# A mixture-of-experts layer on one core: no zero fill of the table of rows, its sums before the last up-projection, and seven output banks begun ahead

## Chip, cores and metric

The kernel runs on one core of a Trainium2 chip. The metric is the device time of one execution in microseconds (us). The core has five engines with queues of their own: TensorE (PE in the profile; PEld is its weight load), VectorE (DVE), ScalarE (ACT), GpSimd (POOL) and SyncE (SP), which here only issues transfers (DMAs). ACT and POOL issue DMAs too; such an instruction stands in the engine's own program, in order with its computing instructions.

## The reference

One transformer layer over 512 latent tokens of width 1024, beside 256 context tokens: a mixer (neighbourhood attention and a gated delta net), then a mixture of 32 experts of which each token uses 4, then a final norm. The part that the change touches is the last:

```python
logits = xf @ w_router + b_router
top_val, top_idx = lax.top_k(logits, 4)
gates = softmax(top_val)
# for each token and each of its four experts e:
hb = x @ w1[e] + b1[e];  gate, up = hb[:1024], hb[1024:]
gate = min(gate, 7);  up = clip(up, -7, 7)
act = (up + 1) * gate * sigmoid(1.702 * gate)
y[token] += gates[token, e] * (act @ w2[e] + b2[e])
# then
out = rmsnorm(x1 + g2 * y, final_norm_w)
```

## The kernel before, in words

**Stages.** The first stage, the mixer, lasts to about 745 us. Its instructions are ordered by a scheduler that plans with a model of the times. PE multiplies in three products of split operands (`hh`, `hl` with `whi`, `wlo`), which ACT and DVE make from each weight block: ACT writes the rounded part `whi` (L29) and DVE the remainder `wlo` (L30). The weight blocks of the mixer are loaded by ACT's own queue (L1050). The delta net's part of it (L1380 to L1600) makes a triangular matrix per block (`AT`, L1413), sends it through memory (L1420, L1456), inverts it on DVE in 30 small steps (L1462, L1463), merges halves on PE (L1491, L1500, with `X` copied by ACT between them, L1493) and then runs 12 steps in a row (`step`); other projections fill PE between the steps.

**Experts.** The second stage takes the 32 experts in an order by their number of tokens. From `e = 2` on, every engine keeps the order of the program (`strict`). Expert `e` has gate weights `g`, up weights `u` and down weights `w2`, each as four chunks of 1 MB, and SP loads them in the order of `Stream.order`: `g` of `e`, `w2` of `e - 1`, `u` of `e`. Ten buffers (`RAWB`) hold the chunks; a chunk is asked for when the chunk ten places ahead of it has been used (`pump`). So all of this stage hangs on one stream of 384 chunks, and of eight more of kind `y`.

**Table of rows.** The weighted result of each expert (`weighted`) is written to the table `y4d` of 2048 rows (512 tokens, four slots each) by a scatter that POOL issues (`scatter`, L591). This is done for experts 0 to 29. Experts 30 and 31, both small (at most 64 tokens), never go through the table: `last(t, n, i)` adds them from `yl[i]` by a product with a 0/1 matrix. Rows of slots that belong to experts 30 and 31, or to tokens over an expert's capacity, must read as zero, so nine transfers on ACT's queue write zeros to the whole table in the mixer (L1434 to L1438), behind the stores of `v`.

**The end.** The table is read back as eight `y` chunks, two for each quarter `t` of the tokens; `rows_of(t)` adds them to the residual `x1`: one add on POOL and three on DVE for each `t`. In the stream they stand as four (quarters 0, 1) ahead of the last `u` and four (quarters 2, 3) ahead of the last `w2`. The output has eight banks (`t`, `n`), each a sum of four products on PE: `second` (bias), `last` with `i = 0` (expert 30), `rest` (`x1` times the identity) and `last` with `i = 1` (expert 31). Seven banks get the first two ahead of the last `w2` and `rest` between its third and fourth chunk; the eighth bank (3, 1) shares its room with the result of `w2` and is made after it. Then come the squares (ACT), the norm's factor (DVE), the scaling and four stores on SP's queue. Last stands a branch (`overflow`) for tokens over capacity, which is not entered with these inputs.

Of the kernel before, what the change touches and what calls it, by code (L numbers as in the profile page):

```python
# [38 lines left out]
class Stream:  # L39
# [3 lines left out]
    def __init__(self, tc, ctx, w1, w2, y4d, NE):  # L43
        self.tc, self.nc = tc, tc.nc
        self.pool = ctx.enter_context(tc.tile_pool(name="moe_raw", bufs=RAWB, side="right"))
        self.w1, self.w2, self.y4d = w1, w2, y4d
        self.raw = {}
        self.order = []
        for e in range(NE + 1):
            if e < NE:  # L50
                self.order += [(e, "g", c) for c in range(4)]
            if e:
                self.order += [(e - 1, "w2", c) for c in range(4)]
            if e < NE:
                self.order += [(e, "u", c) for c in range(4)]
        for i, t in ((-4, 2), (-12, 0)):
            self.order[i:i] = [(t + c // 2, "y", c % 2) for c in range(4)]
        self.loaded = self.used = 0
        self.eidx = None
        self.reg = {}  # L60
# [83 lines left out]
def moe(tc, ctx, cst, release, rps, rt, rtp, h2, hx, h2d, x1d, y4d, modd, w1, b1, w2, b2, fn_d, out, NE=32):  # L144
# [100 lines left out]
    def turn(e, src, q, dst):  # L245

        p = bank("tr").rearrange("p (k s) -> p k s", k=4)
# [9 lines left out]
    def turned(e, src, dst):  # L257
        for q in range(1 if small(e) else 2):
            turn(e, src, q, dst)
# [41 lines left out]
    tlast = sb.tile([128, 2, 4], F32, name="tlast")  # L301
    fnb = sb.tile([128, 1024], F32, name="fnb")
# [255 lines left out]
    GS, AT, TA, YS = {}, {}, {}, []  # L558
# [20 lines left out]
    def transp(e):  # L579
# [3 lines left out]
        turned(e, AT.pop(e), [t])  # L583
        TA[e] = [t]

    def scatter(e, y):
# [6 lines left out]
        for q in YS:  # L593
            tc.declare_no_dep(s.ins, q.ins, reason="rows of other slots")
        YS.append(s)
# [8 lines left out]
    def overflow(n, ovi, rowd, gatd):  # L604

        with tc.If(n > 0):
            with tc.For_i(0, n) as j:
                e = nc.values_load(ovi[0:1, bass.ds(j, 1)], min_val=0, max_val=31)
                with ExitStack() as s2:
# [56 lines left out]
                    tf = lp.tile([128, 4], F32, name="tf")  # L666
                    nc.vector.tensor_copy(tf[:, 0:1], tk)
                    for t in range(1, 4):
                        nc.vector.tensor_scalar(tf[:, t:t + 1], tf[:, 0:1], -128.0 * t, None, op0=OP.add)
                    ot = lp.tile([128, 4, 128], F32, name="ot")  # L670
                    for t in range(4):
                        nc.vector.tensor_scalar(ot[:, t], iot, tf[:, t:t + 1], None, op0=OP.is_equal)
                        for i in range(2):
                            p = bank("y")
                            v = slice(512 * i, 512 * i + 512)
                            nc.tensor.matmul(p, ot[:, t], y[:, v], start=True, stop=True)
                            nc.vector.tensor_tensor(x1[:, t, v], x1[:, t, v], p, op=OP.add)
# [3 lines left out]
    def second(t, n):  # L681
        LP[t, n] = bank(("h", "h", "tr", "y")[t])
        PE.matmul(LP[t, n], Gt[:, 128 * t:128 * t + 128], bs[:, 512 * n:512 * n + 512], start=True, stop=False)
# [6 lines left out]
    def rest(t, n):  # L690
        PE.matmul(LP[t, n], ident, x1[:, t, 512 * n:512 * n + 512], start=False, stop=False)
# [7 lines left out]

    for e in range(NE + 1):  # L700
        strict[0] = e >= 2
# [40 lines left out]
        if e:  # L742
# [5 lines left out]
            else:  # L748
                weighted(e - 1, p, yl[0])
                turned_()  # L750
                for t in range(2):
                    rows_of(t)
        nxt = e + 2 if 1 <= e < NE - 2 else None
        pu = mm(XT.pop(e), e, "u", (lambda c: gather(nxt) if c == 1 else None) if nxt else None)
        ahead(e + 1, "g")
        up(e, pu)
        if 1 <= e and e + 4 < NE:
            fetch(e + 4)

    transp(NE - 1)  # L760
    for t in range(2, 4):
        rows_of(t)
    p = [bank("y")]
    seven = [(t, n) for t in range(4) for n in range(2)][:7]
    for q in seven:
        second(*q)
        last(*q, 0)

    def early(c):
        if c == 2:  # L770
            for q in seven:
                rest(*q)

    p = mm(TA.pop(NE - 1), NE - 1, "w2", early, p)
# [70 lines left out]
def consts(tc, ctx):  # L845
# [15 lines left out]
    c["zero"] = zr = sb.tile([128, 120], F32, name="zero")  # L861
    nc.gpsimd.memset(zr, 0.0)
# [52 lines left out]
def mixer(tc, ctx0, ctx, ctx2, cst, I, rope_d, mask_d, modd, x1d, h2d, y4d, rt, dbg=None, upto=99):  # L915
# [1053 lines left out]
```

## Time and profile before

| | us |
|---|---|
| median of 3 runs (least, most) | 1869.85 (1867.04, 1880.26) |
| the profiled execution | 1870.34 |
| its span | 1868.5 |
| PE busy (share of the span) | 1701.3 (91%) |
| DVE busy | 986.8 (53%) |
| ACT busy | 623.6 (33%) |
| POOL busy | 272.9 (15%) |
| mean rate of the DMAs | 308 GB/s |
| zeros to the table | 8 transfers of 1020 KB and one of 32 KB |

The profiled execution lies 0.5 us above the median, and 1.8 us of its time lie around the span. The share of busy time is a mean over stages with different limits, so the rows are read stage by stage. A matmul's end is modelled, so the distance between starts tells more than its duration. In a timeline, neighbouring instructions of one kind are merged, with their count behind an x; in brackets stands how long the engine was idle ahead and what ended it.

### The profile page before, as it was taken

The numbers are of one execution on the slowest core, as the hardware profiler recorded it, in microseconds if no ns is written. First come the engines' busy times: TensorE is split into PE (matmuls) and PEld (weight loads), VectorE is DVE, ScalarE is ACT, GpSimd is POOL, SyncE is SP. The second block draws the span as 40 slices with busy tenths as digits, with TensorE's granted clock in tenths as the row PEclk, the third lists the DMA queues.
The fourth block names the chain that finished last, engine by engine and source line by source line (L and its number), as shares of the span: only waits on it lengthen the run. The fifth ranks groups of instructions, "written<-read, shape, count | busy, mean of one in ns | idle before, by whom it ended". The sixth has DMA issues, their size and how long they took to land. (4 is left out here: it accounts for less than half of the span.)

```text
span 1868.5 us, 25316 instructions
## 1 busy us (share of the span) xinstructions
PE 1701.3 (91%) x9475; PEld 1047.0 (56%) x9475; DVE 986.8 (53%) x1562; ACT 623.6 (33%) x851; POOL 272.9 (15%) x257
## 2 busy tenths in 40 slices
PE   5979896699999989789999999999999999999966
PEld 1556674587877768435455446554455645554412
DVE  2456792694556685834345337453354633553434
ACT  2534443333335542113224225232233432342201
POOL 0132100233200151310111011010110101100011
PEclk9989998799999999899999999999999999999989
DMA  7647749767488652999999999999999999999993
GB/s 254 206 128 225 212 117 269 204 161 181 134 201 210 190 180 102 351 366 409 410 409 409 409 408 408 399 398 402 408 398 402 400 384 409 405 409 383 410 410 134
DMA packets 280995, 574.68 MB, mean 308 GB/s; under 512 B 79150, under 2 KB 142082, under 8 KB 280740
## 3 DMA queue, kind: packets, MB, share of 16 engines
q1 hardware_dynamic: 185576, 488.25, 70.3%
q10 hardware_dynamic: 88237, 67.88, 12.8%
q0 software_dynamic: 7056, 16.91, 2.4%
q8 instruction: 76, 1.25, 0.3%
q14 instruction: 50, 0.41, 0.1%
HBM read 529.68 MB, written 51.02 MB: 311 GB/s over the span
## 5 line engine op out<-in xcount | busy, mean ns | idle before, releaser
L170 DVE TENSOR_TENSOR B<-raw,whi 128x2048 fp32r<-128x2048 f32 x120 | 273.5, 2290 | 170.6 <-ACT whi L170 170.3
L170 PE MATMUL y<-raw,at 128*64 128x512 f32 (+1 forms) x1024 | 336.7, 594 | 3.7 <-DMA raw<-in_w_dram 3.7
L170 ACT ACTIVATE whi<-raw 128x2048 fp32r<-128x2048 f32 x120 | 229.3, 1915 | 151.0 <-DMA raw<-in_w_dram 111.3
L170 PE MATMUL h<-raw,xts 128*64 128x512 f32 x1024 | 238.6, 608 | 13.7 <-DMA raw<-in_w_dram 13.6
L170 PEld LDWEIGHTS y<-raw,at 128*64 128x64 f32 (+1 forms) x1024 | 132.3, 163 | 190.3 <-issue 182.6
L1067 PE MATMUL pj<-hh,whi 128*128 128x512 f32 (+3 forms) x432 | 164.9, 384 | 21.7 <-ACT whi L29 16.9
L591 POOL DMA_INDIRECT y4d<-yy,rows x30 | 50.3, 1676 | 813.9 <-DVE yy L170 755.4
L170 DVE TENSOR_SCALAR h<-h 128x512 f32<-128x512 f32 x96 | 65.0, 694 | 184.6 <-PE h L170 184.6
L1068 PE MATMUL pj<-hl,whi 128*128 128x512 f32 (+3 forms) x432 | 161.0, 376 | 0.0
L1070 PE MATMUL pj<-hh,wlo 128*128 128x512 f32 (+3 forms) x432 | 159.1, 377 | 0.3 <-DVE wlo L30 0.3
L170 PEld LDWEIGHTS h<-raw,xts 128*64 128x64 f32 x1024 | 68.9, 139 | 151.0 <-issue 132.7
L170 PE MATMUL h<-whi,xth 128*128 128x512 f32 x480 | 137.1, 407 | 10.3 <-ACT whi L170 10.1
L170 PE MATMUL h<-B,xth 128*128 128x512 f32 x480 | 133.3, 399 | 6.1 <-DVE B L170 5.8
L170 PE MATMUL h<-whi,xtl 128*128 128x512 f32 x480 | 131.3, 395 | 0.0
L29 ACT ACTIVATE whi<-raw 128x512 fp32r<-128x512 f32 (+1 forms) x105 | 64.9, 625 | 183.3 <-PE pj L1068 83.2
L30 DVE TENSOR_TENSOR wlo<-raw,whi 128x512 fp32r<-128x512 f32 (+1 forms) x105 | 77.3, 741 | 90.5 <-ACT whi L29 90.3
L170 PEld LDWEIGHTS h<-whi,xth 128*128 128x128 f32 x480 | 86.3, 188 | 41.7 <-ACT whi L170 24.8
L170 PEld LDWEIGHTS h<-B,xth 128*128 128x128 f32 x480 | 87.9, 188 | 37.1 <-DVE B L170 18.0
L1067 PEld LDWEIGHTS pj<-hh,whi 128*128 128x128 f32 (+1 forms) x432 | 82.5, 191 | 46.8 <-ACT whi L29 18.2
L170 DVE SCALAR_TENSOR_TENSOR yy<-y,gates,g2b 128x512 f32<-128x512 f32 x32 | 24.0, 751 | 157.3 <-PE y L170 155.6
L170 ACT ACTIVATE at<-tr 128x512 f32<-128x512 f32 x48 | 27.0, 596 | 236.7 <-PE tr L170 236.7
L170 PEld LDWEIGHTS h<-whi,xtl 128*128 128x128 f32 x480 | 90.1, 188 | 21.7
(494 smaller groups left out, 2405.7 us busy)
## 6 DMA issues: line engine op xcount, KB each, us to landing
raw<-in_w_dram SPq DMA_DIRECT2D x384, 1024.0 KB
raw<-in_w_in_dram ACTq DMA_DIRECT2D x44, 512.0 KB
raw<-in_w_mod_dram ACTq DMA_DIRECT2D x32, 512.0 KB
raw<-in_w_mod_dram SPq DMA_DIRECT2D x16, 512.0 KB
raw<-y4d SPq DMA_DIRECT2D x8, 1024.0 KB
y4d<-zero ACTq DMA_DIRECT2D x8, 1020.0 KB
kk<-nkd SPq DMA_DIRECT2D x16, 384.0 KB
gad<-st ACTq DMA_DIRECT2D x16, 256.0 KB
```

Of the source, the lines that this page charges most:

```text
L29: nc.scalar.activation(hi, src, AF.Copy)
L30: nc.vector.tensor_tensor(lo, src, hi.bitcast(F32), op=OP.subtract)
L170: i = f(*a, **k)
L591: s = nc.gpsimd.indirect_dma_start(out=dst, out_offset=bass.IndirectOffsetOnAxis(ap=rows[:, k:k + 1], axis=0), in_=y, in_offset=None, boun ...
L1067: nc.tensor.matmul(p, h, mh(k), start=k == 0, stop=False)
L1068: nc.tensor.matmul(p, h, ml(k), start=False, stop=False)
L1070: nc.tensor.matmul(p, l, mh(k), start=False, stop=k == kb - 1)
```

## The change

Four things. The nine zero writes of the mixer go, and with them their order behind the stores of `v`. In their place POOL issues two scatters of a tile of zeros (128 x 512, set once) at the end of iteration `e = 3`, to the rows of experts 30 and 31. After the output, POOL scatters the two experts' results to the table, so that the overflow branch finds all rows there and makes its sums anew; the eight copies of the banks to `x1` at the end go. All eight `y` chunks stand ahead of the last `u`, and all four `rows_of` with them. The banks are begun in another order: four (`first`) get `second` and `last` with `i = 0` ahead of the last `u` and `rest` behind it; three (`then`) get all three products between `u` and `w2`; the eighth is summed in the room of `w2`'s result ahead of it and is kept as `x1` by an ACT copy.

```diff
-        for i, t in ((-4, 2), (-12, 0)):
-            self.order[i:i] = [(t + c // 2, "y", c % 2) for c in range(4)]
+        self.order[-8:-8] = [(t, "y", c) for t in range(4) for c in range(2)]
...
+    zero = sb.tile([128, 512], F32, name="zero")
+    nc.gpsimd.memset(zero, 0.0)
...
-        for q in YS:
+        for q in YS + (ZS if e < NE - 2 or zero else []):
             tc.declare_no_dep(s.ins, q.ins, reason="rows of other slots")
-        YS.append(s)
+        (ZS if zero else YS).append(s)
...
+    first, then = [(0, 0), (0, 1), (2, 0), (3, 0)], [(1, 0), (1, 1), (2, 1)]
...
                 weighted(e - 1, p, yl[0])
                 turned_()
-                for t in range(2):
+                pu, pt, pl = [bank("h")], bank("tr"), [bank("y")]
+                for q in first:
+                    second(*q)
+                    last(*q, 0)
+                for t in range(4):
                     rows_of(t)
...
+        if e == 3:
+            for i in range(2):
+                scatter(NE - 2 + i, zero, True)
...
-    transp(NE - 1)
-    for t in range(2, 4):
-        rows_of(t)
-    p = [bank("y")]
-    seven = [(t, n) for t in range(4) for n in range(2)][:7]
-    for q in seven:
+    for q in first:
+        rest(*q)
+    transp(NE - 1, pt)
+    for q in then:
         second(*q)
         last(*q, 0)
-    def early(c):
-        if c == 2:
-            for q in seven:
-                rest(*q)
-    p = mm(TA.pop(NE - 1), NE - 1, "w2", early, p)
+        rest(*q)
+    second(3, 1, pl[0])
+    last(3, 1, 0)
+    rest(3, 1, stop=True)
+    ACT.activation(x1[:, 3, 512:1024], pl[0], AF.Copy)
+    p = mm(TA.pop(NE - 1), NE - 1, "w2", None, pl)
     weighted(NE - 1, p, yl[1])
...
-    for q in seven:
+    for q in sorted(first + then):
         last(*q, 1)
-    second(3, 1)
-    last(3, 1, 0)
-    rest(3, 1)
+    rest(3, 1, start=True)
     last(3, 1, 1)
...
-    for (t, n), p in LP.items():
-        if n:
-            ACT.activation(x1[:, t, 512 * n:512 * n + 512], p, AF.Copy)
-        else:
-            DVE.tensor_copy(x1[:, t, 512 * n:512 * n + 512], p)
+    for i in range(2):
+        scatter(NE - 2 + i, yl[i])
...
-        d = nc.scalar.dma_start(vd[128 * t:128 * t + 128], v)
-        for i in range(2 * t, min(2 * t + 2, 9)):
-            z = cst["zero"][:, None, :].to_broadcast([128, 17, 120]) if i < 8 else cst["zero"][:, 0:64]
-            z = nc.scalar.dma_start(dap(y4d, i * 2040, [[16384, 128], [120, 17], [1, 120]] if i < 8 else [[16384, 128], [1, 64]]), z)
-            issue_behind(tc, z.ins, d.ins)
+        nc.scalar.dma_start(vd[128 * t:128 * t + 128], v)
```

Lines behind the diff's places shift by a few: the helper's L170 becomes L169, L591 becomes L592, L1493 becomes L1488.

On ACT, in the mixer where four of the zero writes stood (`vd` is the store of `v`, `whi` the rounded weights that PE waits for), before:

```order
L1378 DMA dgd<-st 128x512
L1433 DMA vd<-v 128x512
L1437 DMA y4d<-zero 128x17x120 x2
L1433 DMA vd<-v 128x512
L1437 DMA y4d<-zero 128x17x120 x2
L29 ACTIVATE whi<-raw 128x512 x2
L1357 ACTIVATE st<-pj 128x512
L1050 DMA raw<-in_w_in_dram 128x4x256
```

and now:

```order
L1378 DMA dgd<-st 128x512
L1433 DMA vd<-v 128x512
L1491 COPY T<-Z 32x8x32
L1492 COPY T<-Z 32x8x32
L1491 COPY T<-Z 32x8x32
L1492 COPY T<-Z 32x8x32
L1433 DMA vd<-v 128x512
L29 ACTIVATE whi<-raw 128x512
L1050 DMA raw<-in_w_in_dram 128x4x256
```

The four zero writes between the two `vd` stores and the next `whi` are gone; four copies of the merge have moved up in their place.

On PE, from the `w2` of expert 30 (`y<-raw`, its result banks) to the `u` of expert 31 (`h<-raw`); `h<-B`, `tr<-B`, `y<-B` are `second`, and `yl,oh` is `last`. Before:

```order
L170 MATMUL y<-raw,at 64x512 x16
L170 MATMUL tr<-ident,xtl 96x128 x4
L170 MATMUL h<-raw,xts 64x512 x16
L170 MATMUL h<-bb,bsel 128x512
L170 MATMUL tr<-ident,sg 128x128 x4
L170 MATMUL h<-B 128x512
```

and now:

```order
L169 MATMUL tr<-ident,xtl 96x128 x4
L169 MATMUL h<-B 128x512
L169 MATMUL h<-yl,oh 128x512
L169 MATMUL h<-B 128x512
L169 MATMUL h<-yl,oh 128x512
L169 MATMUL tr<-B 128x512
L169 MATMUL tr<-yl,oh 128x512
L169 MATMUL y<-B 128x512
L169 MATMUL y<-yl,oh 128x512
L169 MATMUL h<-raw,xts 64x512 x16
```

Four pairs of `second` and `last` now stand ahead of `u`.

On PE, from the last bank begun to the end (`y<-raw` is now the `w2` of expert 31, `A,ident` is `rest`). Before:

```order
L170 MATMUL y<-yl,oh 128x512
L170 MATMUL y<-raw,at 64x512 x12
L170 MATMUL h<-A,ident 128x512 x4
L170 MATMUL tr<-A,ident 128x512 x2
L170 MATMUL y<-A,ident 128x512
L170 MATMUL y<-raw,at 64x512 x4
L170 MATMUL h<-yl,oh 128x512 x4
L170 MATMUL tr<-yl,oh 128x512 x2
L170 MATMUL y<-yl,oh 128x512
L170 MATMUL y<-B 128x512
```

and now:

```order
L169 MATMUL y<-B 128x512
L169 MATMUL y<-yl,oh 128x512
L169 MATMUL y<-A,ident 128x512
L169 MATMUL y<-raw,at 64x512 x16
L169 MATMUL h<-yl,oh 128x512 x4
L169 MATMUL tr<-yl,oh 128x512 x2
L169 MATMUL y<-yl,oh 128x512
L169 MATMUL y<-A,ident 128x512
L169 MATMUL y<-yl,oh 128x512
```

The seven `rest` products have left `w2`, and behind it the eighth bank needs two products in place of four. On SP, three of the four output stores now stand behind the overflow branch; all four stood ahead of it.

## Rows read from the trace of the kernel before

**Rows 1.** Page, part 2: the whole span in 40 slices of 46.7 us

```profile
PE   5979896699999989789999999999999999999966
...
DMA  7647749767488652999999999999999999999993
GB/s 254 206 128 225 212 117 269 204 161 181 134 201 210 190 180 102 351 366 409 410 409 409 409 408 408 399 398 402 408 398 402 400 384 409 405 409 383 410 410 134
```

**Rows 2.** Busy time by stretch: PE, PEld, DVE, ACT, POOL, PEclk, DMA share, GB/s

```profile
300.00:310.00 10.00, 3.89 (x78) 2.82 (x76) 0.00 (x0) 2.21 (x5) 0.00 (x0) 0.99 1.10 270
310.00:320.00 10.00, 0.00 (x0) 0.00 (x0) 0.00 (x0) 0.00 (x0) 0.00 (x0) 0.50 1.16 287
...
340.00:350.00 10.00, 7.37 (x84) 6.05 (x85) 2.37 (x5) 3.11 (x7) 1.85 (x2) 0.63 1.00 250
```

**Rows 3.** Timeline, ACT and its queue: start, us, operation [idle before]

```profile
284.25 0.33 ACTq L1378 DMA_DIRECT2D dgd<-st  x1
...
305.18 6.06 ACTq L1437 DMA_DIRECT2D y4d<-zero  x2
311.34 3.93 ACTq L1433 DMA_DIRECT2D vd<-v  x1
315.31 5.30 ACTq L1437 DMA_DIRECT2D y4d<-zero  x2
320.66 1.15 ACT L29 ACTIVATE whi<-raw 128x512 fp32r<-128x512 f32 x2 [17.65 <-DMA vd<-v]
...
335.62 4.87 ACTq L1437 DMA_DIRECT2D y4d<-zero  x2
```

**Rows 4.** Timeline, PE, in the same stretch

```profile
321.35 0.79 PE L1067 MATMUL pj<-hh,whi 128*128 128x512 f32 x1 [16.21 <-ACT whi L29]
...
322.36 0.63 PE L1070 MATMUL pj<-hh,wlo 128*128 128x512 f32 x1
...
327.47 0.40 PE L1067 MATMUL pj<-hh,whi 128*128 128x512 f32 x1
...
342.63 0.26 PE L1500 MATMUL dn<-Z,X 32*32 32x32 f32 x2 [8.84 <-ACT X L1493]
...
360.53 0.43 PE L1565 MATMUL sc<-Sbd,KQ 128*64 128x128 f32 x2 [2.38 <-POOL KQ L1556]
```

**Rows 5.** Busy time by stretch, as in rows 2: filler, experts, last loads

```profile
430.00:745.00 315.00, 292.63 (x2590) 233.53 (x2591) 192.47 (x400) 130.25 (x246) 65.84 (x54) 0.99 0.63 173
757.00:1828.00 1071.00, 1025.90 (x4100) 543.38 (x4100) 508.25 (x544) 318.31 (x288) 127.54 (x74) 0.99 1.02 402
1828.00:1840.00 12.00, 12.00 (x38) 3.87 (x39) 5.92 (x4) 0.00 (x0) 2.70 (x1) 1.00 0.33 132
```

**Rows 6.** Timeline, SP: the four output stores

```profile
1853.54 8.29 SPq L802 DMA_DIRECT2D out_dram<-xf  x4
```

**Rows 7.** Timeline, PE, at the end

```profile
1797.42 1.94 PE L170 MATMUL y<-raw,at 128*64 128x512 f32 x8 [0.64 <-DMA raw<-in_w_dram]
...
1810.93 7.39 PE L170 MATMUL h<-raw,xts 128*64 128x512 f32 x24 [11.01 <-DMA raw<-in_w_dram]
...
1820.48 0.50 PE L170 MATMUL h<-bb,bsel 128*128 128x512 f32 x1
...
1822.97 0.48 PE L170 MATMUL h<-B 96*128 96x512 f32 x1
...
1833.32 5.37 PE L170 MATMUL y<-raw,at 128*64 128x512 f32 x24
1838.62 3.70 PE L170 MATMUL h<-A,ident 128*128 128x512 f32 x8
```

**Rows 8.** Timeline, DVE and ACT, at the end

```profile
1846.82 0.75 DVE L170 SCALAR_TENSOR_TENSOR yl<-y,gates,g2s 128x512 f32<-128x512 f32 x1 [12.77 <-PE y L170]
...
1855.01 0.60 ACT L170 ACTIVATE junk<-y 128x512 f32<-128x512 f32 x1 [2.07 <-PEq L606]
```

**Rows 9.** Table of rows: its scatters (ns least, median, most; first and last start)

```profile
L591 POOL DMA_INDIRECT y4d<-yy,rows x30: 989/1018/2825, 832.4 to 1773.0; - x30
```

More of the change, by code (lines that the diff above doesn't have):

```diff
@@ L243, in parts, with turn @@
         DVE.tensor_tensor(lo, src, hi.bitcast(F32), op=OP.subtract)
-    def turn(e, src, q, dst):
-        p = bank("tr").rearrange("p (k s) -> p k s", k=4)
+    def turn(e, src, q, dst, p=None):
+        p = (bank("tr") if p is None else p).rearrange("p (k s) -> p k s", k=4)
         for k in range(4):
@@ L255, in turn, with turned @@
             ACT.activation(dst[0][:, 4 * q:4 * q + 4], p, AF.Copy)
-    def turned(e, src, dst):
+    def turned(e, src, dst, p=None):
         for q in range(1 if small(e) else 2):
-            turn(e, src, q, dst)
+            turn(e, src, q, dst, p)
     def gather(e, src=None):
@@ L556, in mm @@
         return p
-    GS, AT, TA, YS = {}, {}, {}, []
+    GS, AT, TA, YS, ZS = {}, {}, {}, [], []
     def gate(e, p):
@@ L577, in up, with transp @@
         AT[e] = s
-    def transp(e):
+    def transp(e, p=None):
         t = wk3.tile([128, 8, 128], F32, name="at", bufs=2)
@@ L582, in transp, with scatter @@
             t = t[:, 0:4].rearrange("p a (b s) -> p (a b) s", b=2)
-        turned(e, AT.pop(e), [t])
+        turned(e, AT.pop(e), [t], p)
         TA[e] = [t]
-    def scatter(e, y):
+    def scatter(e, y, zero=False):
         k = column(e)
@@ L665, in overflow, with second @@
                         nc.vector.scalar_tensor_tensor(y[:, v], p, ga, g2b[:, v], op0=OP.mult, op1=OP.mult)
[L666 to L677, printed above, removed]
+                    nc.gpsimd.indirect_dma_start(out=y4d[:, :], out_offset=bass.IndirectOffsetOnAxis(ap=rw[:, 0:1], axis=0),
+                                                 in_=y, in_offset=None, bounds_check=2047, oob_is_err=False)
     LP = {}
-    def second(t, n):
-        LP[t, n] = bank(("h", "h", "tr", "y")[t])
-        PE.matmul(LP[t, n], Gt[:, 128 * t:128 * t + 128], bs[:, 512 * n:512 * n + 512], start=True, stop=False)
+    def second(t, n, p=None, stop=False):
+        LP[t, n] = p = bank(("h", "h", "tr", "y")[t]) if p is None else p
+        PE.matmul(p, Gt[:, 128 * t:128 * t + 128], bs[:, 512 * n:512 * n + 512], start=True, stop=stop)
     def last(t, n, i):
@@ L688, in last, with rest @@
         PE.matmul(LP[t, n], ohT[i][h, t, :], yl[i][h, :], start=False, stop=i == 1)
-    def rest(t, n):
-        PE.matmul(LP[t, n], ident, x1[:, t, 512 * n:512 * n + 512], start=False, stop=False)
+    def rest(t, n, start=False, stop=False):
+        PE.matmul(LP[t, n], ident, x1[:, t, 512 * n:512 * n + 512], start=start, stop=stop)
     def rows_of(t):
@@ L698, in rows_of @@
         stream.pump()
+    first, then = [(0, 0), (0, 1), (2, 0), (3, 0)], [(1, 0), (1, 1), (2, 1)]
     for e in range(NE + 1):
+        pu = None
         strict[0] = e >= 2
@@ L750, in moe @@
                 turned_()
-                for t in range(2):
+                pu, pt, pl = [bank("h")], bank("tr"), [bank("y")]
[3 more added lines that the diff above has]
+                for t in range(4):
                     rows_of(t)
         nxt = e + 2 if 1 <= e < NE - 2 else None
-        pu = mm(XT.pop(e), e, "u", (lambda c: gather(nxt) if c == 1 else None) if nxt else None)
+        pu = mm(XT.pop(e), e, "u", (lambda c: gather(nxt) if c == 1 else None) if nxt else None, pu)
         ahead(e + 1, "g")
@@ L833, in moe @@
     with tc.If(ovt[0] > 0):
+        nc.sync.dma_start(x1, x1d.rearrange("(t p) d -> p t d", p=128))
         for t in range(4):
+            for k in range(4):
+                r = stream.pool.tile([128, 2, 1024], F32, name="raw")[:, 0]
+                nc.sync.dma_start(r, y4d[512 * t + 128 * k:512 * t + 128 * k + 128, :])
+                nc.vector.tensor_tensor(x1[:, t], x1[:, t], r, op=OP.add)
+            for n in range(2):
+                p, v = bank("h"), slice(512 * n, 512 * n + 512)
+                nc.tensor.matmul(p, Gt[:, 128 * t:128 * t + 128], bs[:, v], start=True, stop=True)
+                nc.vector.tensor_tensor(x1[:, t, v], x1[:, t, v], p, op=OP.add)
             squares(t, [x1[:, t, 512 * n:512 * n + 512] for n in range(2)])
@@ L860, in consts @@
     nc.vector.memset(o1, 1.0)
-    c["zero"] = zr = sb.tile([128, 120], F32, name="zero")
-    nc.gpsimd.memset(zr, 0.0)
     c["sb"] = sb
```

## The prediction, made before the changed kernel ran

> **What bounds the kernel now.** I read the page's 40 slices first, because the kernel has two stages with different limits [rows 1]. From the 17th slice on the DMAs are busy for 9 tenths or more and move about 400 GB/s: that is the stream of expert weights. Ahead of it they move 102 to 269 GB/s, and PE has 9s and 8s with a hole in the 7th slice (a 6). Then I read busy time by stretch. From 757 to 1828 us the DMA share is 1.02 at 402 GB/s [rows 5]: the experts wait for their weights, so this stage ends a fixed time after its stream starts. In the mixer from 430 to 745 us PE is busy for 292.63 of 315 us [rows 5]: there PE is the limit, and what PE gains earlier passes through to the start of the stream. So two places decide: the mixer's hole, and what follows the last load.
>
> The hole is at 300 to 350 us. PE is idle for all of 310 to 320 us while the DMA share stands at 1.16 [rows 2]. The timelines say why. ACT needs 6.06 us to issue two zero writes, 3.93 us for a store of `v` behind them and 5.30 us for two more zero writes; only then, at 320.66, it makes the `whi` that PE has waited 16.21 us for [rows 3, 4]. An issue of the same queue took 0.33 us at 284 us [rows 3]. At 335.62 the last two zero writes hold ACT for 4.87 us, and PE waits 8.84 us for `X` [rows 3, 4]. At both places ACT has computing to do that stands behind an issue.
>
> At the end PE, not the stream, is last. The DMA share falls to 0.33 from 1828 to 1840 us while PE is busy throughout [rows 5]. PE had idled 11.01 us ahead of the last `u`, since four `y` chunks pass in front of it [rows 7].
>
> **The zero writes go.** I build the gain M of the mixer from four terms.
>
> A: PE's 16.21 us, less the 1.15 us of the two `whi` that ACT must make anyway [rows 3, 4]: 15.1 us. Bounds: 11.4 us if only the zeros' own issues (6.06 + 5.30) come back, 16.2 if the `whi` are ready in time.
>
> B: of the 8.84 us, the 4.87 us of issue, since the rest is the copies and the `X` that stand behind it: 4.8 us. Bounds 0 and 8.8.
>
> C: the clock. After the first gap the products from 321.35 us on, ten of them, show 0.63 us each (one row of them stands), against 0.40 at 327.47 [rows 4]; the granted clock in the gap was 0.50 [rows 2], which is 1.2 GHz. After the second gap eight more show 0.63. 18 × 0.2 = 3.6 us (rounding 0.23 down, as matmuls overlap). Bounds 0 and 4.1.
>
> D: loads of the first delta net steps come behind the zeros: from 340 to 350 us the DMA share is still 1.00 [rows 2], and PE waits for the load-fed `KQ` at 360.53, 2.38 us [rows 4]. I take those 2.4 us; the bounds are 0 and 7, three waits of that size.
>
> M = 15.1 + 4.8 + 3.6 + 2.4 = 25.9 us, bounds 11.4 and 36.1.
>
> The Trainium skill says on the page "DMA: Bandwidth & Descriptors", section "Issuing engines are not separate DMA queues", that issuing from several engines saves only the sequencer's time of issue, "which is usually small relative to the DMA itself". By that the ACT program would get back little, and the trace does not agree at this place: issues behind a full queue took 3 us each. The rival that the rule makes is the third below.
>
> The scheduler plans the mixer anew without the zeros, and the rows on ACT show four copies pulled ahead. That order has no price in the trace; I count it at nothing, with a few us either way inside the bounds of M.
>
> **The stream.** All eight `y` chunks and the four `u` and `w2` chunks are the same bytes as before. New are two scatters of at most 64 rows of 4 KB each, 0.52 MB at 402 GB/s [rows 5]: 1.3 us at most. POOL's issue costs 0.99 to 2.83 us each [rows 9] and lies beside the stream; behind them on POOL stand only gathers for four experts later. I take 1.3 us.
>
> **The end.** Four chunks more pass ahead of the last `u`: 4.19 MB at 402 GB/s are 10.4 us [rows 5]. Before, `u` ends at 1820.48 + 0.50 = 1820.98 [rows 7], and the last square starts at 1855.01 [rows 8], 34.0 us later. Let me count this distance anew, with prices from rows 7. A pair `second`, `last` costs 1.48 us (seven pairs from 1822.97 to 1833.32). A `rest` costs 0.9 us (eight halves, four products, in 3.70). A chunk of `w2` costs 1.8 us (three in 5.37). Now, behind `u`:
>
> - `rest` of four banks: 3.6
> - transposes: 0.4
> - three banks of 1.48 + 0.9: 7.1
> - the eighth bank: 2.4
> - its ACT copy, which `w2` waits for since it takes the same bank: 0.6 as the square of this size [rows 8] and 0.2 for the hand-over: 0.8
> - `w2`, all landed by then: 7.2
> - `yl` on DVE: 0.8 [rows 8]
> - from `yl` to the last square, before 1855.01 − 1847.57 = 7.4 [rows 8], now without one pair: 5.9
>
> The sum is 28.2 us, so PE wins 5.8 us and loses 10.4 us: the end comes 4.6 us later. DVE's wait for `u`, `up`, is hidden behind the four `rest`. The four sums `rows_of` run while PE waits for `u`; their last chunk lands four chunks ahead of `u`'s last. The four early pairs (5.9 us) lie in the wait ahead of `u`, which grows from 11.01 us by 10.4. PE restarts there at the low clock as it does now (24 products in 7.39 us, against 5.37 at full speed [rows 7]), so that loss stands on both sides. Bounds of the end: +2 (no hand-over and half of the bytes ahead) to +9 (the low clock lasts through `u` and the first `rest`).
>
> The scatter of `yl[0]` is issued by POOL behind its last add and puts 0.26 MB beside the last loads: 0.65 us at most, of which I count none, as PE is behind the loads. That of `yl[1]` runs beside the tail; POOL's scaling behind it starts 10 us later. Without the eight copies DVE and ACT stop earlier, but the stores end last. Three of the four stores now stand behind the branch on SP: the first store starts at 1853.54 and the four take 8.29 us [rows 6], so the branch has some 5 us in which the next tile is not ready. If that cover were gone, it costs at most the 6.7 us from the last store's issue (1861.83) to the span's end (1868.5), in which the branch lies now.
>
> **Sum.** 1870.34 (the profiled execution, 1.8 us of it around the span and 0.5 above the median) − 25.9 + 1.3 + 4.6 = 1850.3. I say 1850.
>
> **Rivals.**
>
> 1. *Everything in the hole comes back.* M = 36.1. For it: DVE shows no work at all from 300 to 320 us and ACT 2.21 us [rows 2], so neither would be the next limit there. Against: the other DMAs of this stretch must then fit into less time. 1870.3 − 36.1 + 5.9 = 1840.
>
> 2. *Only the zeros' own issues come back.* M = 11.4 to 16; the second wait, the loads and the clock stay because other loads crowd the queue. 1870.3 − 14 + 5.9 = 1862.
>
> 3. *The other side: ACT stays held.* If the 16.21 us hang on the `vd` stores and weight loads and not on the zeros, as the profile's own releaser ("DMA vd<-v") has it, ACT's queue is still full, or the lead is lost to the next wait. With M below 5.9 the change is slower; with M = 2 the time is 1874. Against: the eight large zero writes are 8.2 MB, where the whole 7th slice moved 12.6 MB (269 GB/s for 46.7 us [rows 1]), and an issue took 0.33 us just before [rows 3]. The skill's sentence above, that issue time is small, belongs to this case.
>
> 4. *The end is dearer.* PE waits about 15 us before `u`, and the clock stays low into the `rest` block, or `w2` waits for scatter bytes: end +9, 1870.3 − 25.9 + 10.3 = 1855.
>
> That the change doesn't do what it says is not a rival: the order shows no zero write left.
>
> **Chances.** Forecast (M from 20 to 31) 0.45, rival 1 0.20, rival 2 0.20, rival 3 0.08, rival 4 0.07. A measurement here tells 1% from no change, 18.7 us, so "faster" begins below 1851.2. The forecast's span of 1845 to 1856 lies half on each side: 0.25 faster, 0.20 same. Rival 1 is faster; rivals 2 and 4 are same; rival 3 is same up to 1888, and I leave it 0.04 beyond that for a worse plan of the mixer. Faster 0.46, same 0.50, slower 0.04. The range reaches from rival 1 with a good end (1838) to rival 2 with its least M and a dear end (1866).
>
> **What would show it.** In the mixer: no issue on ACT's queue above 1 us between 290 and 345 us, PE's wait for `whi` gone, the stretch of the experts, with its DMA share of 1.02, begun at about 731 us in place of 757. At the end: PE idle for 12 to 16 us ahead of `u`, then busy without a gap of over 1 us until `w2` ends, about 21 us behind `u`; the last square 28 us behind `u` in place of 34. I am wrong if that start has moved by less than 15 us, if PE waits for `w2`'s chunks, or if the span ends more than 15 us behind the last square (13.5 now).

## The result, and the profile after

The changed kernel took 1847.26 us (median of 4 runs, 1843.59 to 1849.09), the kernel before in the same rounds 1872.46 us; the ratio is 0.986, with a 95% interval of 0.9819 to 0.990. In later rounds, as `after_again` below, it was 0.9867 (0.9846 to 0.9887). The profiled execution is the slowest of the four, 1849.09 us with a span of 1847.2.

The hole in the mixer is closed but for one gap. Busy time by stretch of the changed kernel, with the columns of [rows 2]:

```profile
300.00:310.00 10.00, 10.00 (x167) 8.17 (x166) 8.89 (x20) 6.41 (x15) 0.00 (x0) 1.00 0.79 213
310.00:320.00 10.00, 6.42 (x110) 5.08 (x109) 6.21 (x21) 4.44 (x9) 1.85 (x2) 0.83 0.85 244
340.00:350.00 10.00, 8.18 (x80) 7.36 (x81) 9.65 (x17) 1.26 (x2) 5.70 (x6) 1.00 0.75 172
```

PE is busy for 24.6 of these 30 us, where it was 11.3 [rows 2]. Between 310 and 320 us a gap of 3.6 us is left, ended by a load. On ACT's queue no issue from 290 to 350 us is over 0.42 us now; rows of 6.06, 5.30 and 4.87 us stood there [rows 3]. The longest in the changed kernel:

```profile
290.11 0.42 ACTq L1433 DMA_DIRECT2D vd<-v  x1
```

The stream starts sooner, but not in the same manner. SP's queue before, with the weight loads (`in_w_dram`) and the constants of the experts' stage, `g2b` among them:

```profile
750.48 0.61 SPq L310 DMA_DIRECT2D g2b<-modd  x1
...
757.22 2.06 SPq L83 DMA_DIRECT2D raw<-in_w_dram  x2
```

and in the changed kernel:

```profile
724.32 4.60 SPq L82 DMA_DIRECT2D raw<-in_w_dram  x6
729.09 5.97 SPq L311 DMA_DIRECT2D g2b<-modd  x1
735.10 2.50 SPq L312 DMA_DIRECT2D fnb<-in_final_norm_w_dram  x1
737.65 3.37 SPq L315 DMA_DIRECT2D g2s<-modd  x2
743.13 77.67 SPq L82 DMA_DIRECT2D raw<-in_w_dram  x26
```

The third weight load is issued at 724.32 us instead of 757.22. But the constants, which stood ahead of that load, now stand behind eight weight loads, and SP needs 5.97, 2.50 and 3.37 us to issue them there.

The end, first on PE (with `y<-raw,at` of 1771.23 the last chunk of expert 30's `w2`):

```profile
1771.23 1.94 PE L169 MATMUL y<-raw,at 128*64 128x512 f32 x8 [0.61 <-DMA raw<-in_w_dram]
...
1775.98 0.49 PE L169 MATMUL h<-B 96*128 96x512 f32 x1 [2.25 <-DVE B L169]
...
1784.26 2.07 PE L169 MATMUL y<-yl,oh 64*128 64x512 f32 x2
1794.96 9.92 PE L169 MATMUL h<-raw,xts 128*64 128x512 f32 x32 [8.63 <-DMA raw<-in_w_dram]
1804.81 0.50 PE L169 MATMUL h<-bb,bsel 128*128 128x512 f32 x1
...
1819.22 7.09 PE L169 MATMUL y<-raw,at 128*64 128x512 f32 x32 [0.69 <-ACT A L169]
```

then the last square on ACT (PEq is PE's sequencer):

```profile
1833.13 0.60 ACT L169 ACTIVATE junk<-y 128x512 f32<-128x512 f32 x1 [0.53 <-PEq L607]
```

`u` ends at 1804.81 + 0.50 = 1805.31 us, and the last square starts 27.8 us later; it was 34.0.

For the comparisons that follow I cut the span of each kernel in four, at events that each of them has: **A**, from its start to the issue of the third weight load; **B**, from there to the start of the last chunk of `w2` of expert 30 on PE; **C**, from there to the start of the last square; **D**, from there to the end. (These letters are stretches of the span; the terms A to D of the prediction's M are something else.)

| kernel | A | B | C | D | span |
|---|---|---|---|---|---|
| before | 757.2 | 1040.2 | 57.6 | 13.5 | 1868.5 |
| changed | 724.3 | 1046.9 | 61.9 | 14.1 | 1847.2 |
| difference | -32.9 | +6.7 | +4.3 | +0.6 | -21.3 |
| predicted | -25.9 | +1.3 | +4.6 | 0 | -20.0 |

### The profile page after: what moved, and what is told of

It is laid out like the page before. It is cut to its first block, busy times and chain, and to the rows that moved or that the text cites. A ratio compares the mean times of both kernels' runs of the same rounds, so it can differ in the third digit from the quotient of the medians.

```text
span 1847.2 us, 25328 instructions
## 1 busy us (share of the span) xinstructions
PE 1704.7 (92%) x9477; PEld 1048.1 (57%) x9477; DVE 991.4 (54%) x1558; ACT 622.3 (34%) x848; POOL 276.0 (15%) x261
## 5 line engine op out<-in xcount | busy, mean ns | idle before, releaser
L169 DVE TENSOR_TENSOR B<-raw,whi 128x2048 fp32r<-128x2048 f32 x120 | 273.6, 2290 | 172.0 <-ACT whi L169 171.8
L169 PE MATMUL y<-raw,at 128*64 128x512 f32 (+1 forms) x1024 | 336.6, 594 | 4.2 <-DMA raw<-in_w_dram 2.1
L169 ACT ACTIVATE whi<-raw 128x2048 fp32r<-128x2048 f32 x120 | 229.3, 1915 | 152.4 <-DMA raw<-in_w_dram 111.7
L169 PE MATMUL h<-raw,xts 128*64 128x512 f32 x1024 | 238.5, 608 | 11.0 <-DMA raw<-in_w_dram 11.0
L169 PEld LDWEIGHTS y<-raw,at 128*64 128x64 f32 (+1 forms) x1024 | 132.6, 163 | 190.8 <-issue 181.2
L592 POOL DMA_INDIRECT y4d<-yy,rows x30 | 50.2, 1675 | 814.3 <-DVE yy L169 814.3
L169 DVE TENSOR_SCALAR h<-h 128x512 f32<-128x512 f32 x96 | 65.3, 695 | 183.9 <-PE h L169 183.9
L169 PEld LDWEIGHTS h<-raw,xts 128*64 128x64 f32 x1024 | 69.1, 139 | 149.3 <-issue 131.4
L169 PE MATMUL h<-whi,xth 128*128 128x512 f32 x480 | 136.8, 406 | 11.3 <-ACT whi L169 11.0
L169 PE MATMUL h<-B,xth 128*128 128x512 f32 x480 | 133.4, 399 | 6.1 <-DVE B L169 5.9
L169 PE MATMUL h<-whi,xtl 128*128 128x512 f32 x480 | 131.4, 395 | 0.0
L30 DVE TENSOR_TENSOR wlo<-raw,whi 128x512 fp32r<-128x512 f32 (+1 forms) x105 | 83.6, 800 | 64.0 <-ACT whi L29 63.8
L169 PEld LDWEIGHTS h<-whi,xth 128*128 128x128 f32 x480 | 86.2, 188 | 42.9 <-ACT whi L169 25.9
L169 ACT ACTIVATE at<-tr 128x512 f32<-128x512 f32 x48 | 27.1, 596 | 245.2 <-PE tr L169 233.9
L169 PEld LDWEIGHTS h<-B,xth 128*128 128x128 f32 x480 | 87.7, 188 | 36.8 <-DVE B L169 18.2
L169 DVE SCALAR_TENSOR_TENSOR yy<-y,gates,g2b 128x512 f32<-128x512 f32 x32 | 24.0, 751 | 157.2 <-PE y L169 155.5
L169 PEld LDWEIGHTS h<-whi,xtl 128*128 128x128 f32 x480 | 90.1, 188 | 21.9
L1067 PEld LDWEIGHTS pj<-hh,whi 128*128 128x128 f32 (+1 forms) x432 | 82.1, 190 | 32.9 <-ACT zb L1252 4.5
```

What stands on the lines that cost most here:

```text
L30: nc.vector.tensor_tensor(lo, src, hi.bitcast(F32), op=OP.subtract)
L169: i = f(*a, **k)
L592: s = nc.gpsimd.indirect_dma_start(out=dst, out_offset=bass.IndirectOffsetOnAxis(ap=rows[:, k:k + 1], axis=0), in_=y, in_offset=None, boun ...
L1067: nc.tensor.matmul(p, h, mh(k), start=k == 0, stop=False)
```

## The experiments

Two questions were open. Why did the zero writes cost 33 us: since issues held ACT's program (the prediction's theory), or since the DMA engines were busy with them, whatever queue they come from? And where did the 12 us go that B, C and D cost? A to C are from one profiled execution of each kernel; the ratio is from all of its runs.

| kernel | ratio to before (95% interval) | A | B | C |
|---|---|---|---|---|
| `zeros_off`: mixer's part alone | 0.9825 (0.9777 to 0.9873) | 719.4 | 1046.7 | 57.3 |
| `end_only`: end alone | 1.0009 (0.9989 to 1.0029) | 756.7 | 1038.5 | 61.9 |
| `zeros_narrow`: zeros in 240-B runs | 1.0213 (1.0163 to 1.0263) | 798.9 | 1041.3 | 57.9 |
| `zeros_sp`: zeros from SP | 1.0021 (0.9993 to 1.005) | 754.9 | 1046.0 | 57.6 |
| `zeros_pool`: zeros from POOL | 1.0065 (1.0034 to 1.0096) | 761.7 | 1044.4 | 57.6 |
| `zeros_spread`: zeros between the steps | 0.9897 (0.9865 to 0.993) | 735.7 | 1043.3 | 57.6 |
| `zero_ring`: changed, zeros from a ring | 0.9841 (0.9781 to 0.9901) | 726.4 | 1039.5 | 61.4 |
| `y_back`: changed, `y` of 2, 3 behind `u` | 0.9806 (0.9744 to 0.9868) | 730.1 | 1044.9 | 54.1 |
| `after_again`: the changed kernel | 0.9867 (0.9846 to 0.9887) | 725.8 | 1046.2 | 62.0 |
| `no_banks`: changed, no banks ahead | 0.9935 (0.991 to 0.996) | 722.4 | 1046.9 | 77.6 |
| `y_back_ring`: both mends | 0.9793 (0.9771 to 0.9815) | 725.1 | 1038.9 | 54.3 |
| `end_before_ring`: end of before, ring | 0.9836 (0.9808 to 0.9865) | 722.2 | 1037.9 | 57.9 |

**The two parts apart.** `zeros_off` is the kernel before with this in the mixer, and the two zero scatters:

```diff
+        if e == 3:
...
+            for i in range(2):
+                scatter(NE - 2 + i, zero, True)
...
-        for i in range(2 * t, min(2 * t + 2, 9)):
...
-            issue_behind(tc, z.ins, d.ins)
```

> The kernel before without the nine zero writes in the mixer and with the two zero scatters at e = 3; the end is that of before. Theory (the zero writes held ACT, the stream of weights starts earlier, and it loses some 6 us of that at its start and to the scatters): the third weight load is issued at about 724 us as in the changed kernel (757.22 before), and the time is 1870 - 33 + 6 = 1843 us, 1839 to 1848. It would then be some 4 to 5 us faster than the changed kernel. Rival (part of the gain came from the end, or from a plan of the mixer that only the changed kernel has): third load at 735 us or later, time 1854 us or more.

It took 1838.8 us, a little under the theory's span; A is 719.4, and it shows the same late constants as the changed kernel (B 1046.7). All of the gain comes without the new end. `end_only` is the changed kernel with the zero writes back in the mixer and without the zero scatters:

> The changed kernel with the nine zero writes back on ACT's queue in the mixer and without the zero scatters, so only the end and the order of the y chunks differ from before. Theory: the u product ends 10 us later than before, 28 us instead of 34 lie between it and the last square, and the time is 4 to 6 us more than before, 1874 to 1876 us. Rival (the end gains, since seven banks are begun ahead of or right behind u): 1866 us or less.

It took 1873.26 us beside 1870.52, under the theory's 1874 to 1876; the ratio's interval holds 1, so the times show no loss, but no gain either, and the rival falls. C is 4.3 us longer, as in the changed kernel. PE of `end_only`:

```profile
1795.16 1.94 PE L169 MATMUL y<-raw,at 128*64 128x512 f32 x8 [0.63 <-DMA raw<-in_w_dram]
...
1818.88 9.91 PE L169 MATMUL h<-raw,xts 128*64 128x512 f32 x32 [8.07 <-DMA raw<-in_w_dram]
1828.71 0.50 PE L169 MATMUL h<-bb,bsel 128*128 128x512 f32 x1
```

and its last square on ACT:

```profile
1857.05 0.60 ACT L169 ACTIVATE junk<-y 128x512 f32<-128x512 f32 x1 [0.54 <-PEq L605]
```

From the end of `u` at 1829.21 to the last square there are 27.8 us, as the sum has it. So the new end lengthens C by what the sum gave; that the whole kernel is slower by it is not clear of the noise.

**Queue or engines.** `zeros_narrow` halves the runs (the contiguous pieces of a transfer) and doubles the packets on ACT's queue, with the same bytes:

```diff
-            z = cst["zero"][:, None, :].to_broadcast([128, 17, 120]) if i < 8 else cst["zero"][:, 0:64]
-            z = nc.scalar.dma_start(dap(y4d, i * 2040, [[16384, 128], [120, 17], [1, 120]] if i < 8 else [[16384, 128], [1, 64]]), z)
+            z = cst["zero"][:, None, 0:60].to_broadcast([128, 34, 60]) if i < 8 else cst["zero"][:, 0:64]
+            z = nc.scalar.dma_start(dap(y4d, i * 2040, [[16384, 128], [60, 34], [1, 60]] if i < 8 else [[16384, 128], [1, 64]]), z)
```

> The kernel before with the same zero bytes on the same queue at the same place, but in runs of 240 B instead of 480 B, so twice as many packets. Theory (an issue holds ACT until the queue has room for its packets, so what counts is how long the packets take to drain): the issues behind a full queue grow from about 3 to 4 or 6 us each, PE's wait for whi grows from 16 us to 25 or more, time up by 10 to 30 us. Rival (the bytes on the DMA engines count): the same 8.2 MB, waits within 3 us of before, time 1867 to 1873 us.

It took 1913.24 us, 42.7 more than before where the theory had 10 to 30; A is 41.7 us later. Two zero writes now take 10.46 us to issue, where they took 6.06, and the store behind them 9.74, where it took 3.93 [rows 3]:

```profile
317.37 10.46 ACTq L1437 DMA_DIRECT2D y4d<-zero  x2
327.92 9.74 ACTq L1433 DMA_DIRECT2D vd<-v  x1
```

So the bytes alone don't set the cost; shorter runs of the same bytes cost more. What they cost the DMA engines stands in part 3 of each page, in ACT's queue `q10` (packets, MB, share of sixteen engines' span), before:

```profile
q10 hardware_dynamic: 88237, 67.88, 12.8%
```

changed:

```profile
q10 hardware_dynamic: 70557, 59.49, 11.1%
```

and with 240-B runs:

```profile
q10 hardware_dynamic: 105645, 67.88, 15.3%
```

The zeros' 17680 packets took 0.128 x 1868.5 - 0.111 x 1847.2 = 34 us of all sixteen engines. That is the size of what A gained (27 to 38 us in the kernels without zeros in the mixer). With 240-B runs they took another 0.153 x 1911.6 - 0.128 x 1868.5 = 53 us, and A lost 42: the same order, not the same number.

That run doesn't say which it is, held issues or busy engines, as both grew. `zeros_sp` and `zeros_pool` do: in the code only the engine that issues the zeros is changed (`nc.gpsimd` stands for `nc.sync` in `zeros_pool`), and the scheduler plans the mixer anew.

```diff
-            z = nc.scalar.dma_start(dap(y4d, i * 2040, ...
+            z = nc.sync.dma_start(dap(y4d, i * 2040, ...
```

> The kernel before with the same zero writes in runs of 480 B issued by SP instead of ACT, behind the same stores of v in the plan. Theory (holding ACT's own computing is what costs): whi comes in time, PE's wait of 16 us goes, the issues of several us stand on SP's queue, and what SP loads behind them comes later; the third weight load is at 730 to 747 us and the time 1845 to 1862 us. Rival (the DMA engines were overloaded from 290 to 345 us by 8.2 MB of zeros, whatever queue they come from): PE waits as long for other tiles, the third load is at 752 us or later, the time 1865 us or more.

It took 1873.62 us, and A is 754.9: the rival's time, although no zero write held ACT. SP is held instead of ACT, and PE waits 9.73 us for a load. SP's queue:

```profile
301.22 14.43 SPq L1437 DMA_DIRECT2D y4d<-zero  x4
```

and PE:

```profile
328.28 0.26 PE L1491 MATMUL dn<-Z,OA 32*32 32x32 f32 x2 [9.73 <-DMA Z<-td]
```

This doesn't yet part the two, since the loads of the delta net stand on SP's own queue. POOL has next to nothing to compute there.

> The kernel before with the same zero writes in 480-B runs issued by POOL, whose own queue has next to nothing to compute between 290 and 345 us. Theory A (a queue that is full holds what stands behind an issue in the same program; ACT's weights and SP's loads are needed there, POOL's work is not): PE's waits for whi and Z go, third weight load at 724 to 732 us, time 1838 to 1852 us. Theory B (the 17408 packets of 480 B take the DMA engines 31 ns each in the trace of before, which is 34.4 us of all sixteen, in a stretch where their share is about 1; every load there is late by that, whatever queue issues the zeros): third load at 750 us or later, time 1862 us or more.

It took 1884.97 us: slower than the kernel before (1876.6 in the same rounds), with A at 761.7. POOL issued all eight zero writes in 10.31 us and was through:

```profile
283.13 10.31 POOL L1437 DMA_DIRECT2D y4d<-zero  x8
```

Yet SP, which issued none of them, was held for 18.05 us by one store of 256 KB and for 10.45 us by another; before, the issue of the first had taken 0.56 us:

```profile
289.36 18.05 SPq L1428 DMA_DIRECT2D ptd<-P__1642  x1
307.46 4.05 SPq L1476 DMA_DIRECT2D Z<-td  x1
311.60 10.45 SPq L1428 DMA_DIRECT2D ptd<-P__1646  x1
```

and ACT waited 18.45 us for the load of `Z` that stood between them:

```profile
311.12 0.40 ACT L1496 COPY T<-Z 32x256 f32<-32x256 f32 x1 [18.45 <-DMA Z<-td]
```

So here a long issue was a sign that the DMA engines were behind, on whichever queue the work for them had come. The theory that ACT's held program is the cause falls: without its zero writes the time stays. That the queues are not apart the Trainium skill states in "DMA: Bandwidth & Descriptors", section "Issuing engines are not separate DMA queues": all of them run "on the same 16 DMA engines and interleave with each other, regardless of the engine that started them". These two runs agree, at 1.0021 and 1.0065 of before. From POOL the zeros went in 2208 packets of some 3.8 KB, by part 3 of its page, and took 0.041 x 1877.1 - 0.024 x 1868.5 = 32 us of the engines: an eighth of the packets took as long, so their number isn't what costs.

`zeros_spread` keeps the zeros on ACT, one behind each of nine steps of the delta net:

```diff
+        c = nc.scalar.copy(Vn, px)
+        if n < 9:
...
+            z = nc.scalar.dma_start(dap(y4d, n * 2040, ...
+            issue_behind(tc, z.ins, c.ins)
```

> The kernel before with the same nine zero writes on ACT's queue, but one behind each of the first nine steps of the delta net, a stretch in which PE is the limit and the DMA share is 0.63. Theory (the place is what costs, both by A and by B): no issue of a zero write over 1 us, third weight load within 6 us of the kernel without zero writes (719.44), time 1836 to 1848 us. Rival (34 us of DMA time have to be paid wherever they stand, since the steps wait for their loads): third load at 740 us or later, time 1858 us or more.

It took 1854.77 us, between the two. No issue of a zero write is long, as the rows of the table `y4d` show (ns least, median, most; first and last start):

```profile
L1574 ACTq DMA_DIRECT2D y4d<-zero x9: 338/408/1167, 319.6 to 456.0; - x9
```

but A is 735.7, some 16 us later than `zeros_off` had it in its run. The mean share of 0.63 was of another stretch: [rows 5] begin at 430 us, and the zeros stand from 319.6 to 456.0. PE lost most between 360 and 400 us. In `zeros_spread`:

```profile
360.00:400.00 40.00, 31.58 (x527) 28.48 (x526) 33.06 (x78) 11.35 (x25) 11.14 (x14) 0.87 0.78 198
```

and in `zeros_off`:

```profile
360.00:400.00 40.00, 37.76 (x671) 32.31 (x671) 33.08 (x79) 16.80 (x37) 10.36 (x15) 1.00 0.58 148
```

PE is busy for 6.2 us less there. So the place bought somewhat over half; which of the steps' loads pays the rest I did not settle. Nor do these runs part the zeros from the plan: each kernel's mixer is ordered anew, and among the kernels without zeros in it A differs by 11 us.

**The start of the stream.** In the changed kernel the scheduler put the constants behind eight weight loads. The semaphores that this load waits for are others too (before, then changed; `DMAHW` are those of DMAs):

```
L310 DMA g2b<-modd 128x1024 [waits DMAHW2_49]
L311 DMA g2b<-modd 128x1024 [waits DMAHW0_49,DVE_49,DMAHW1_49,PE_49,Pool_49]
```

With the new tile of zeros (2 KB in each partition) `g2b` waits for three engines. `zero_ring` takes the zeros from the ring of `yy` (its two buffers, used in turn) instead:

```diff
-    zero = sb.tile([128, 512], F32, name="zero")
-    nc.gpsimd.memset(zero, 0.0)
...
         if e == 3:
+            zero = xp.tile([128, 1024], F32, name="yy", bufs=2)[:, 0:512]
+            POOL.memset(zero, 0.0)
```

> The changed kernel with its tile of zeros taken from the ring of yy at e = 3 instead of a place of its own. In the changed kernel the load of g2b waits for DVE, PE and POOL and stands behind eight weight loads; with the ring it waits for a DMA alone, as before, and stands ahead of them. Theory (the tile's 2 KB moved g2b, fnb and g2s to places that come free later, and their 1.3 MB then run beside the first weights): the stretch from the third weight load to 20 MB later is 3 to 5 us shorter, time 1841 to 1845 us against 1847. Rival (the slow start of the stream has another cause, as the rows of the gathers): 1846 to 1850 us.

It took 1842.9 us, within the theory's span. SP's queue of `zero_ring`, with the constants early again:

```profile
719.70 0.66 SPq L309 DMA_DIRECT2D g2b<-modd  x1
...
726.44 52.77 SPq L82 DMA_DIRECT2D raw<-in_w_dram  x17
```

and its last `w2` chunk of expert 30 on PE:

```profile
1765.98 1.94 PE L169 MATMUL y<-raw,at 128*64 128x512 f32 x8 [0.62 <-DMA raw<-in_w_dram]
```

B is 1039.5 us against 1046.9 and 1046.2 in the two profiles of the changed kernel. Two more pairs differ in the ring alone, `y_back` and `y_back_ring` (1044.9 and 1038.9), `zeros_off` and `end_before_ring` (1046.7 and 1037.9). So without the tile B is 6 to 9 us shorter in all three; A of the three changed by +1.4, -5.0 and +2.8, so some of it may be given back there. By the times no pair is clear of the noise: the intervals of each overlap, and `end_before_ring` has the higher ratio of its pair. How the tile holds the constants back is not shown either: `g2b`, `fnb` and `g2s` lie at the same addresses in the kernel before, the changed one and `zero_ring`, so the theory's "places that come free later" are not theirs. The two zero scatters, which are in all of these, cost nothing that shows: B with them and the ring is not above the 1040.2 of before. B of `zeros_sp`, `zeros_pool` and `zeros_spread` is 3 to 6 us over that too, with the constants early; why, I leave open.

**The end.** `no_banks` is the changed kernel with the code of before behind `u`, and all `y` chunks still ahead of it.

> The changed kernel with the code of before behind the last u (seven pairs behind u, rest between the chunks of w2, the eighth bank last), all eight y chunks still ahead of u. Theory (the banks begun ahead shorten the way from u to the last square by 6 us, in the sum 34.0 to 28.2): the way is 33.5 to 34.5 us again and the time 5 to 7 us more than the changed kernel, about 1853 us. Rival (PE's restart at the low clock or the wait ahead of u swallow the banks' gain): within 3 us of the changed kernel.

It took 1861.76 us, 13.3 more than the changed kernel in the same rounds, and C is 77.6 us: about twice the loss that the theory expected. PE of `no_banks`:

```profile
1793.01 7.06 PE L169 MATMUL h<-raw,xts 128*64 128x512 f32 x24 [21.23 <-DMA raw<-in_w_dram]
...
1808.22 2.07 PE L169 MATMUL h<-yl,oh 64*128 64x512 f32 x2
...
1823.86 6.68 PE L169 MATMUL y<-raw,at 128*64 128x512 f32 x24
```

and its busy time by stretch:

```profile
1796.00:1804.00 8.00, 6.34 (x27) 1.58 (x23) 1.83 (x2) 0.00 (x0) 0.00 (x0) 1.00 0.77 306
1804.00:1806.00 2.00, 1.03 (x6) 0.82 (x7) 0.79 (x2) 0.31 (x1) 0.00 (x0) 1.00 0.34 135
1806.00:1826.00 20.00, 20.00 (x26) 5.53 (x27) 0.00 (x0) 0.29 (x1) 0.00 (x0) 0.50 0.03 11
```

The same place in the kernel before:

```profile
1815.00:1821.00 6.00, 5.70 (x25) 1.51 (x21) 0.00 (x0) 0.00 (x0) 0.00 (x0) 1.00 1.03 410
1821.00:1833.00 12.00, 10.41 (x25) 3.75 (x25) 9.55 (x8) 0.60 (x1) 5.81 (x2) 1.00 0.84 334
```

PE idles 21.23 us ahead of `u`, and the granted clock is back at 1.00 from 1796 us on. Then it falls a second time: from 1806 to 1826 us the pairs run at 0.50, the lower level of 1.2 GHz, though PE is busy throughout. Ahead of that fall PE was busy for 6.34 of 8 and 1.03 of 2 us; before, it was busy for 5.70 of 6 us ahead of the same gap of 1.6 us, and the same pairs ran at full clock. What made the clock fall I did not settle. A pair takes 2.73 us (1808.22 to 1810.95) instead of 1.48 [rows 7], seven of them 18.5 instead of 10.35, and three chunks of `w2` 6.6 instead of 5.3, from start to start. So 9.5 of the 15.7 us by which C is longer are the low clock, and the other 6.2 are what the theory expected of the banks. The four pairs ahead of `u` in the changed kernel are dearer than I took them (10.35 us for the four from 1775.98, at the low clock), but they lie in the wait, and behind `u` the clock is whole.

`y_back` puts the `y` chunks of quarters 2 and 3 back behind `u`, and the `rest` of these quarters behind the pairs:

```diff
-        self.order[-8:-8] = [(t, "y", c) for t in range(4) for c in range(2)]
+        for i, t in ((-4, 2), (-12, 0)):
+            self.order[i:i] = [(t + c // 2, "y", c % 2) for c in range(4)]
...
-    for q in first:
+    for q in first[:2]:
         rest(*q)
     transp(NE - 1, pt)
+    for t in range(2, 4):
+        rows_of(t)
...
+    for q in ((2, 0), (2, 1), (3, 0)):
+        rest(*q)
```

> The changed kernel with the y chunks of quarters 2 and 3 back behind the last u (the order of before), the banks begun ahead of u as in the changed kernel, and rest of quarters 2 and 3 moved behind the pairs. Theory (the four chunks cost 10.4 us ahead of u, and PE's 21 us of work between u and the end of w2 are the limit behind it): u ends 10 us earlier, PE waits a few us for the last sums or the last w2 chunk, time 5 to 8 us less than the changed kernel, 1839 to 1843 us. Rival (DVE's sums of quarters 2 and 3 come too late and w2 starts no earlier): 1846 us or more.

It took 1838.01 us, a little under the theory's span; C is 54.1 against 61.9. PE of `y_back`:

```profile
1775.04 1.94 PE L170 MATMUL y<-raw,at 128*64 128x512 f32 x8 [0.62 <-DMA raw<-in_w_dram]
...
1788.70 2.07 PE L170 MATMUL y<-yl,oh 64*128 64x512 f32 x2
1790.70 8.28 PE L170 MATMUL h<-raw,xts 128*64 128x512 f32 x32
...
1812.54 1.98 PE L170 MATMUL y<-A,ident 128*128 128x512 f32 x4 [1.54 <-DVE A L170]
1815.21 7.09 PE L170 MATMUL y<-raw,at 128*64 128x512 f32 x32 [0.69 <-ACT A L170]
```

`u` starts at 1790.70 without a wait of its own, 15.7 us behind the last `w2` chunk of expert 30 (23.7 in the changed kernel). DVE's sums cost PE 1.54 us ahead of the last `rest`, no more; the rival falls.

The last two put the findings together.

> Both mends of the changed kernel together: zeros from the ring, so that g2b, fnb and g2s are loaded ahead of the weights, and the y chunks of quarters 2 and 3 behind the last u. Theory: the terms add, 5 us from the start of the stream and 7.5 us from the end, so 11 to 13 us less than the changed kernel in the same rounds, 1833 to 1837 us where that is 1847. Rival (the two gains overlap, since PE is not ready for u sooner): 1838 us or more.

> The kernel before with no zero writes, the two zero scatters from the ring, and its own end: the mixer's part with the mend, and no part of the end. Theory: 2 to 4 us more than the variant with both mends (its end measured 42.3 us from 10 MB before the stream's end to the last square, against 39.8), 1836 to 1840 us, and 7 to 11 us less than the changed kernel. Rival (the end of the changed kernel is worth keeping as it is): 1845 us or more.

`y_back_ring` took 1832.85 us, 15.6 less than the changed kernel in the same rounds, where 11 to 13 were expected, and the least of all; the intervals of these two don't meet. `end_before_ring` took 1838.37 us, with runs from 1833.46 to 1851.55. It is 5.5 us above `y_back_ring`, where 2 to 4 were expected; the two intervals just meet, but C is 54.3 against 57.9. B and C of both are those of their parts within 2 us.

> The changed kernel once more, on the chip and in the rounds of the three variants that follow, so that they are compared with it directly. Both theories: 0.983 to 0.99 of the kernel before.

That gave 1848.42 us, as expected.

## Why the prediction was right, and where its steps were off

**The time and the sign.** 1850 was forecast and 1847.26 measured. That it is so near is in part luck: two terms were off by much and nearly cancelled. M was 25.9 us and A gave 32.9, outside the 20 to 31 that the forecast stood on; the stream was put at +1.3 and B took +6.7.

**M, terms A to D.** Each wait that I named went: no issue above 0.42 us, no wait for `whi`, ACT's `X` or `KQ`, and the stretch at a clock of 0.50 is at 0.83. But the terms were mis-sized. PE's busy time up to the third weight load, before:

```profile
0.00:430.00 430.00, 349.65 (x2655) 255.17 (x2656) 260.93 (x545) 163.91 (x290) 72.75 (x125) 0.92 0.69 197
430.00:757.20 327.20, 299.68 (x2644) 239.72 (x2645) 201.04 (x441) 133.38 (x252) 67.44 (x55) 0.98 0.63 173
```

and in the changed kernel:

```profile
0.00:430.00 430.00, 375.98 (x3269) 276.81 (x3270) 275.40 (x572) 178.20 (x318) 85.42 (x142) 0.96 0.67 193
430.00:724.30 294.30, 272.05 (x2029) 218.12 (x2029) 188.19 (x404) 118.70 (x224) 54.23 (x38) 0.96 0.61 169
```

PE idles 26.3 us less ahead of 430 us and 5.3 less behind it: 31.6, where the waits of A, B and D came to 22.3. Its busy time shrank by only 1.3 us, where C, the clock, had 3.6.

The cause was wrong too: the waits were added up as if ACT, held by its issues, were the reason, and `zeros_sp` and `zeros_pool` show that it is not. The measure nearer to the cause was in hand, the DMA share of 1.1 to 1.16 [rows 2]: the zeros (8.4 MB, not the 8.2 of the prediction) took 34 us of the engines in a stretch in which they were full. That gives the size and no more, since 53 us of it cost A 42 in `zeros_narrow`, and the same 34 cost some 16 in `zeros_spread`. Rival 1 had the nearest M; my reason against it, that the other DMAs must fit into less time, did not hold, as they did fit. My reading of the Trainium skill's sentence was wrong as well: I took the long issues for a time of issue that ACT pays, and with other issuing engines the time stayed; but small those issues were not, at up to 18.05 us for one.

**The stream.** The zero scatters were put at 1.3 us at most and cost nothing that shows. What B lost was not in the sum. By the three pairs 6 to 9 us of it go with the new tile, with which three loads of constants came to stand behind six more weight loads; that order stood on SP's queue, which the prediction left out there.

**The end.** +4.6 was forecast, +4.3 (C) and +0.6 (D) measured: 27.8 us from `u` to the last square for 28.2. PE idles 8.63 us ahead of `u`, not 12 to 16, since the four early pairs ran at the low clock and began 2.25 us late; that changed nothing, as the wait was longer. `w2` ends 21.0 us behind `u`, as forecast, with no gap above 0.69 us. The branch on SP and the scatters behind the output cost at most the 0.6 us of D. The 5.8 us that the sum gave the banks are the 6.2 that `no_banks` shows beside its low clock; that the old code with all `y` ahead of `u` would take 43.5 us and not 34.0, by a second fall of the clock, the sum could not have.

**The rivals.** Rival 1's M of 36.1 was nearer to the 32.9 of A than the forecast's, but its time of 1840 did not come, since B lost what it did. Rival 2 (only the zeros' own issues come back) would have left A above 741; rival 3 above 751; rival 4 wanted an end of +9. None of these three came. The chances by outcome add up to 0.45 faster and 0.51 same, where 0.46 and 0.50 stand.

## What to carry to other kernels

An issue that takes several us can mean that the DMA engines are full, as it did here; moving it to another queue then moves the wait. So drop the work if you can, and beware of shorter runs; and count what a transfer takes of the engines (its queue's share in part 3 of the page), not only the waits that show. After a change in memory, look at the order and the waits of the first loads of the next stage: a tile of 2 KB came with loads behind a queue. And when work is moved between the last loads, check the granted clock behind them: a second fall of it cost 9.5 us in `no_banks`.

## What the runs showed of the hardware that was not expected

SP was held for 18.05 us by one store of 256 KB while the DMA engines worked off zeros that POOL had issued. The zeros in runs of 480 B took 34 us of sixteen engines for 8.4 MB, and from POOL, in an eighth of the packets, 32; in runs half as long they took some 87. And in `no_banks` PE's granted clock, back at 1.00 behind an idle stretch of 21.23 us, fell again and stayed at 0.50 from 1806 to 1826 us with PE busy throughout, where in the kernel before the same products ran at 1.00.
